# A hybrid decoder layer on one core: an earlier start of a pair's mixing, token-wise squares, sums on VectorE, ordered sigmoids

## The chip, the core and the metric

The kernel runs on one core of one Trainium2 chip. The core has a matrix engine (TensorE, PE in the rows; PEld is its weight load), VectorE (DVE), ScalarE (ACT), GpSimd (POOL) and SyncE (SP), whose queue issues the DMA transfers of this kernel. The metric is the device time of one execution in microseconds (us), lower is better. A profiled execution also leaves a trace, with a span from the first to the last instruction.

## The reference, cut to what matters

One layer over 2048 prompt tokens and 8 x 8 sample tokens, width 1024:

```python
h = rmsnorm(x, norm_mix_w)                     # input norm
rq, rk, rv, rg, hq, hf, hi, hg = split(h @ w_in)
rq, rk = rotary(rq, pos), rotary(rk, pos) * 128 ** -0.5
o_r = head_rmsnorm(chunk_gla(rq, rk, rv, log_gamma)) * silu(rg)      # 4 retention heads
f = lb + (1 - lb) * sigmoid(hf)
o_h = head_rmsnorm(chunk_gla(silu(hq) * c, 1 - f, hi, log(f))) * silu(hg)  # 4 HGRN heads
x = x + concat(o_r, o_h) @ w_out
x = x + square(relu(rmsnorm(x) @ w_up)) @ w_down
y = rmsnorm(x)
```

`chunk_gla` is a causal gated recurrence, computed chunk by chunk: scores inside a chunk, times decays that come from running sums of log f, plus the state carried over. Outputs are y and the states after the last token.

## The kernel before, in words

Tokens lie along the free dimension. They go through the layer in three groups: group 0 (64 sample and 512 prompt tokens, 576 columns), groups 1 and 2 (768 prompt tokens each). The kernel first mixes group after group, and then does the feed-forward of the three groups. Products are made from float32 values split into a rounded high part (a ScalarE copy, L298 for weights, L434 in `cut`) and a low remainder (a VectorE subtraction, L312, L435), three matmuls for each product.

**Pairs.** Inside a group `mix` goes over four pairs, each a retention head with an HGRN head. A pair has a forget block f and a query block q of the HGRN head, a rotary query block rq and key block rk of the retention head (`project`, `project_quads`), then the value blocks (`values`, L1007), and two gate blocks, which are made one pair later, for the last pair at once (`gates`, `gates_quad`). Groups 1 and 2 make two blocks at a time by a Strassen-like scheme of seven products of 12 matmuls (`quad`, L828): the results are collected in two PSUM tiles, ScalarE copies the first, third and fifth product out (L834, L838, L843), and VectorE adds the others (L816). One sum of two SBUF halves (L841) is on GpSimd. The fifth product accumulates onto the bank of the first, so PE has to wait for the copy of L834 before it.

Rotary (L885 to L889): four half-height ScalarE copies swap halves, VectorE multiplies by the cosine, GpSimd by the sine (L888), VectorE adds. Sigmoids of two blocks are taken together in `sigmoids` (L852): ScalarE needs the sigmoid table for them, and the table set that holds both logarithm and exponential is asked for behind them (L854). The request for the set is kept in program order, the two sigmoids are not.

**Mixing.** `mixer` writes a pair's chunk work into an agenda by due times: logarithms (L1137, L1138), running sums on VectorE (L1143), then, for block widths 64, 32, ... 2, exponents on GpSimd (L1159, L1160), exponentials on ScalarE (L1164), products on VectorE (L1170), and matmuls (corners L1241 for the wide blocks, L1184 for narrow ones). Then come transposes (L1298, L1112), outputs and states (L1368 to L1383) and the head norm with the gate (`gate_norm`, L443, L444, L1460 to L1468). Due times count from t0, in ticks: every two matmuls of a projection block and every three of a value block are a tick, and at each tick what is due is written into the program. In the kernel before, t0 is the tick at which rq and rk are done, or the end of the mixing before it.

**Order.** The order of instructions on each engine is decided by the scheduler of the tile framework, which works from the order of writing and its own estimate of times; `keep_in_program_order` pins an instruction, `high_priority` draws it forward. So an instruction's place follows its due time only roughly.

**Output projection and input norm.** `out_proj` multiplies the heads of three pairs with their weights and adds the input (`residual`, L1510, eight blocks), then adds the last pair (L1553). Beside it, `norm_in` of the next group runs by due times: load x block by block, square on ScalarE (L622), add on VectorE (L625), column sums on PE (L604, L605), reciprocal root (L443, L444), load x again, scale it (L655), round it (L657) and subtract (L661).

**Sums of weights.** During group 0 `plan_quads` makes the weights of the seven products: per set of blocks four loads of 128 x 512, four sums on GpSimd (L364), high parts on ScalarE (L369), low parts on VectorE (L372), eight stores; ten sets, the first at tick 110 and then every 80 ticks. During groups 1 and 2 `plan_sums` does the like for the feed-forward in buffers named raw (L1525); there are four of these, which the weight loads also use.

Of the kernel before, what the change touches and what calls it, by code (L numbers as in the profile page):

```python
# [9 lines left out]
F32 = mybir.dt.float32  # L10
# [209 lines left out]
class Kernel:  # L220
# [133 lines left out]
    def plan_quads(self, start, each):  # L354
# [8 lines left out]
        def make(x, name, a, op, b, into):  # L363
            order(nc.gpsimd.tensor_tensor(out=x[into], in0=x[a], in1=x[b], op=op))  # L364
            x[name] = x[into]
# [97 lines left out]
    def build(self):  # L463
        nc, tc, I = self.nc, self.tc, self.I
        with ExitStack() as ctx:
# [46 lines left out]
            for ns, p0, n in GROUPS:  # L512
                g = type("G", (), {})()
                g.i, g.ns, g.p0, g.n, g.T, g.off = len(gs), ns, p0, n, ns + n, off
                off += g.T
                nch = n // C
                first = nch // 2
                g.pieces = [(0, g.T)] if g.T <= 512 else [(0, g.T // 2), (g.T // 2, g.T)]
                g.segs = [list(range(first)), list(range(first, nch))]
                g.scaled = bool(gs)  # L520
                gs.append(g)
            nc.scalar.dma_start(vec, I["vec"])
# [25 lines left out]
            self.mix(gs[1])  # L548
            self.out_proj(gs[1], 1, lambda: self.norm_in(gs[2], pace=6))
            self.plan_sums(sums[NQ:], at)  # L550
# [76 lines left out]

    def norm_in(self, g, start=False, pace=5):

# [19 lines left out]

        def squares(kb):  # L650
            g.sq = self.add_square(g, g.sq, self.x_block(g, kb), nc.vector)

# [49 lines left out]
        if start:  # L702
# [30 lines left out]
    def mix(self, g):  # L733
        nc = self.nc
# [7 lines left out]
        for p in range(H):  # L742
# [3 lines left out]
            if g.scaled and p == 0:  # L746
                self.plan_sides(g)
            (self.project_quads if g.scaled and p else self.project)(g, p, b)
            end = self.mixer(g, p, b, max(self.now, end))
            if g.scaled and p == H - 1:  # L750
                self.gates_quad(g, b)
                for i in range(H - 1):
                    self.later(1 + 14 * i, self.get_heads, g, i)
                    self.later(16 + 14 * i, self.cut_heads, g, i)
            self.values(g, p, b)
            prev = b
        if g.scaled:
            return
        for p in range(H - 1):
            self.later(2 + 18 * p, self.cut_heads, g, p)  # L760
        self.gates(g, prev)

    def plan_sides(self, g):
# [46 lines left out]
    def quad(self, g):  # L810
# [6 lines left out]
        for k, (A, B) in enumerate(QUAD):  # L817
# [21 lines left out]
            elif k == 3:  # L839
                add(s[:, two], ps, s[:, two])  # L840
                nc.gpsimd.tensor_tensor(out=Q[:, two], in0=s[:, two], in1=s[:, one], op=ALU.add)  # L841
            elif k == 4:
# [7 lines left out]
    def sigmoids(self, *pairs):  # L850
        for out, src in pairs:
            self.nc.scalar.activation(out, src, AF.Sigmoid)  # L852
        with self.tc.high_priority():
# [12 lines left out]

    def project_quads(self, g, p, b):

# [12 lines left out]
        self.later(5, forget)  # L881
        self.later(8, lambda: nc.gpsimd.tensor_tensor(out=z[:, :T], in0=z[:, :T], in1=sgq[:, :T], op=ALU.mult))
        for key, r in zip(("rq", "rk"), self.quad(g)):
            xs = self.get()
# [4 lines left out]
            self.later(9, lambda r=r, xs=xs: nc.vector.tensor_tensor(out=r[:, :T], in0=r[:, :T], in1=xs[:, :T], op=ALU.add))  # L889
            b[key] = r  # L890

    def block(self, g):
# [30 lines left out]

    def project(self, g, p, b):
        nc, T = self.nc, g.T
# [38 lines left out]
        self.later(5, lambda: eng.tensor_tensor(out=self.v2(hq, g), in0=z, in1=self.v2(sgq, g), op=ALU.mult))  # L964

        for key in ("rq", "rk"):
            if not start or key == "rk":
# [5 lines left out]
            self.later(9, lambda q=q, xs=xs: nc.vector.tensor_tensor(out=q[:, :T], in0=q[:, :T], in1=xs[:, :T], op=ALU.add))  # L973
            b[key] = q

    def values(self, g, p, b):
# [145 lines left out]
    def mixer(self, g, p, b, t0):  # L1122
# [5 lines left out]
        q, k, f = b["q"], b["k"], b["f"]  # L1128
        rq, rk = b["rq"], b["rk"]
        cols = [slice(n0 + C * c, n0 + C * (c + 1)) for c in range(n)]  # L1130
# [979 lines left out]
```

## Time and profile before

| | |
|---|---|
| Median of three runs | 2606.51 us (2604.39 to 2615.03) |
| Profiled execution | 2608.76 us, its span 2607.0 us |
| PE busy | 2488.5 us, 95% |
| DVE, ACT, POOL busy | 1933.8, 1335.7, 490.3 us |
| Mean granted PE clock | 0.982 |

How to read it: windows give for each stretch its length and the busy time of each engine with its count of instructions, the granted PE clock, the busy share of the DMA engines and GB/s. A row of waits names who waited for whom, the total in us, the times, and the longest. A group row ends with the busy time and the mean ns of one instruction, then the idle time ahead of it. A busy PE row can contain overlap, and a matmul is slower while the granted clock is 0.5.

### The profile page before, as it was taken

To read this page: it belongs to the slowest core of one execution; us is meant where nothing else is said; L and a number is where in the kernel's file an instruction comes from. 1 tells how busy PE (TensorE), PEld (TensorE's weight loads), DVE (VectorE), ACT (ScalarE), POOL (GpSimd) and SP (SyncE) were. 2 spreads that over 40 slices of the span, in tenths; PEclk is the share of its full clock that TensorE was granted. 3 is DMA by queue.
4 is the path that set the end of the run, shared out by engine and by line. 5 is a ranking of instruction groups with operands and counts; after the bars stand their busy time and mean duration, and the time that the engine had idled before them with its cause. 6 is when DMAs were issued, how large, how long until landed. Compare 5 with 4: busy or idle time off the path is not lost.

```text
span 2607.0 us, 41951 instructions
## 1 busy us (share of the span) xinstructions
PE 2488.5 (95%) x16280; PEld 2451.7 (94%) x16280; DVE 1933.8 (74%) x2567; ACT 1335.7 (51%) x1796; POOL 490.3 (19%) x373
## 2 busy tenths in 40 slices
PE   8999879999989999998999999999999999999998
PEld 8989778988979998888999999999999999999998
DVE  6777778665577756656587799875699868668977
ACT  6665644456554454653464555544454435445443
POOL 6455521453340234523000000000000000000000
PEclk9999989999999999998999999999999999999999
DMA  7778688676866687685586876676666546766553
GB/s 262 256 266 278 217 282 309 235 267 235 289 234 206 250 299 252 243 288 211 197 279 217 274 242 203 211 228 217 215 238 212 172 154 218 244 197 223 181 172 108
DMA packets 226952, 605.16 MB, mean 232 GB/s; under 512 B 23489, under 2 KB 65089, under 8 KB 226754
## 3 DMA queue, kind: packets, MB, share of 16 engines
q1 hardware_dynamic: 226610, 602.47, 67.5%
q8 instruction: 128, 2.10, 0.3%
q14 instruction: 70, 0.57, 0.1%
q10 hardware_dynamic: 144, 0.02, 0.0%
HBM read 448.51 MB, written 152.83 MB: 231 GB/s over the span
## 4 chain that ended last, share of the span: by engine, by line
PE 59%; DVE 2%; POOL 2%; issue 2%; ACT 1%; DVEq 0%; POOLq 0%; ACTq 0%
PE pf L1495 25%; PE pj L1495 24%; PE pj L828 4%; PE pj L427 3%; PE pjv L1007 1%; POOL slab L1160 1%; PE mm L1184 1%; POOL slab L1159 1%; PE po L1370 0%; PE mm L1376 0%; PE po L1368 0%; POOL slab L888 0%; DVE slab L889 0%; DVE lo L312 0%; DVE slab L1143 0%
## 5 line engine op out<-in xcount | busy, mean ns | idle before, releaser
L298 ACT CAST hi<-raw 128x1024 fp32r<-128x1024 f32 x392 | 411.9, 1051 | 604.7 <-PE pj L1495 224.8
L1495 PE MATMUL pf<-slab,hi 128*128 128x384 f32 (+1 forms) x2768 | 652.7, 321 | 0.0
L1495 PE MATMUL pj<-slab,hi 128*128 128x384 f32 (+1 forms) x2608 | 618.2, 322 | 0.0
L312 DVE TENSOR_TENSOR lo<-raw,hi 128x1024 fp32r<-128x1024 f32 x392 | 485.6, 1239 | 114.5 <-ACT hi L298 112.3
L1495 PEld LDWEIGHTS pf<-slab,hi 128*128 128x128 f32 x2768 | 480.4, 188 | 0.1
L1495 PEld LDWEIGHTS pj<-slab,hi 128*128 128x128 f32 x2608 | 454.0, 188 | 0.0
L1495 PE MATMUL pf<-slab,lo 128*128 128x384 f32 (+1 forms) x1384 | 443.6, 320 | 0.0
L1495 PE MATMUL pj<-slab,lo 128*128 128x384 f32 (+1 forms) x1304 | 419.6, 322 | 0.6 <-DVE lo L312 0.6
L427 PE MATMUL pj<-slab,hi 128*128 128x288 f32 (+1 forms) x1792 | 364.2, 319 | 15.1 <-DVE slab L1510 10.3
L828 PE MATMUL pj<-slab,unit 128*128 128x384 f32 x1680 | 348.2, 352 | 25.1 <-ACT slab L834 13.2
L828 PEld LDWEIGHTS pj<-slab,unit 128*128 128x128 f32 x1680 | 294.8, 194 | 30.0 <-ACT slab L834 15.1
L427 PEld LDWEIGHTS pj<-slab,hi 128*128 128x128 f32 x1792 | 290.8, 191 | 18.9 <-issue 9.7
L1495 PEld LDWEIGHTS pf<-slab,lo 128*128 128x128 f32 x1384 | 260.2, 188 | 0.0
L1495 PEld LDWEIGHTS pj<-slab,lo 128*128 128x128 f32 x1304 | 245.1, 188 | 0.9 <-DVE lo L312 0.8
L427 PE MATMUL pj<-slab,lo 128*128 128x288 f32 (+1 forms) x896 | 214.0, 319 | 1.1 <-DVE lo L312 1.1
L1007 PE MATMUL pjv<-hi,slab 128*128 128x256 f32 x1024 | 207.1, 294 | 2.7 <-DVE slab L971 2.7
L1007 PEld LDWEIGHTS pjv<-hi,slab 128*128 128x128 f32 x1024 | 170.1, 198 | 4.6 <-DVE slab L971 3.0
L1588 DVE TENSOR_TENSOR slab<-slab 128x768 fp32r<-128x768 f32 (+1 forms) x192 | 166.7, 885 | 8.8 <-ACT slab L1584 4.5
L1584 ACT CAST slab<-slab 128x768 fp32r<-128x768 f32 (+1 forms) x192 | 144.8, 778 | 53.1 <-DVE slab L1595 42.5
L427 PEld LDWEIGHTS pj<-slab,lo 128*128 128x128 f32 x896 | 153.0, 191 | 1.9 <-DVE lo L312 1.5
L1007 PE MATMUL pjv<-lo,slab 128*128 128x256 f32 x512 | 148.3, 290 | 0.0
L1164 ACT ACTIVATE slab<-slab 128x768 f32<-128x768 f32 (+2 forms) x72 | 56.1, 780 | 136.9 <-POOL slab L1160 85.1
(261 smaller groups left out, 3494.2 us busy)
## 6 DMA issues: line engine op xcount, KB each, us to landing
raw<-w SPq DMA_DIRECT2D x264, 512.0 KB, 4.5
ld<-x SPq DMA_DIRECT2D x64, 384.0 KB, 4.0
slab<-u SPq DMA_DIRECT2D x64, 384.0 KB, 4.8
u<-ld SPq DMA_DIRECT2D x60, 384.0 KB, 4.3
ld<-in SPq DMA_DIRECT2D x28, 384.0 KB, 3.9
slab<-w SPq DMA_DIRECT2D x40, 256.0 KB, 5.1
slab<-u SPq DMA_DIRECT2D x32, 288.0 KB, 4.2
u<-ld SPq DMA_DIRECT2D x30, 288.0 KB, 3.3
```

Source lines behind the costliest of these rows:

```text
L298: self.nc.scalar.copy(hi, raw)
L312: self.nc.vector.tensor_tensor(out=lo, in0=self.second.pop(j), in1=hi.bitcast(F32), op=ALU.subtract)
L427: self.nc.tensor.matmul(pj[:, i, :T2], w, a[:, c0:c1], start=j == 0 and q == 0, stop=j == n - 1 and q == 2)
L828: nc.tensor.matmul(ps, w[:, c], a, start=first and kb == q == 0, stop=kb == KB // 2 - 1 and q == 2, skip_group_check=not first)
L1007: nc.tensor.matmul(pj[:, i * 256:(i + 1) * 256], a[:, s:s + C], ww, start=kb == 0 and q == 0, stop=kb == KB - 1 and q == 2)
L1159: nc.gpsimd.tensor_tensor(out=D4[:, :, 0, :], in0=mid, in1=K4[:, :, 0, :], op=ALU.subtract)
L1160: nc.gpsimd.tensor_tensor(out=D4[:, :, 1, :], in0=B4[:, :, 1, :], in1=mid, op=ALU.subtract)
L1164: nc.scalar.activation(x["dd", w][:, a:T], x["dd", w][:, a:T], AF.Exp)
L1184: nc.tensor.matmul(ps[:, j], qk[:, cols[c]], second(qk[:, cols[c]]), start=True, stop=True)
L1495: self.nc.tensor.matmul(*a, **k)
L1584: self.nc.scalar.copy(hi[:, :g.T], B[name][:, :g.T])
L1588: self.nc.vector.tensor_tensor(out=lo[:, :g.T], in0=B[name][:, :g.T], in1=hi.bitcast(F32)[:, :g.T], op=ALU.subtract)
```

## The change

In groups 1 and 2 a pair's mixing begins 16 ticks behind the f and q blocks and no longer behind rq and rk; the due times of what needs rq and rk move back by 4 ticks, and those of the two diagonal sums by 6. In group 0 mixing begins where it did. The two sigmoids of `sigmoids` are pinned in program order, so both stand ahead of the request for the next table set.

The input norm of the next group begins earlier, behind the gate blocks of the last pair (ahead of those in group 0). It reads x once with a chunk's tokens on the partitions (a new input `xt`, the same values laid out anew) into the raw buffers, six loads of 128 x 1024, squares each with the sum along the row (`accum_out`), takes the reciprocal root of a 128 x 6 tile, writes this to a row in DRAM, and reads the row back for all partitions. The eight squares and seven additions in x's column layout, the column sums on PE and the roots of full width go. The scaling of the eight blocks starts with the first residual block, every 18 ticks.

The four sums of each set of `plan_quads` move from GpSimd to VectorE, and the sets run from tick 100 every 66 ticks. The sum of two halves in `quad` moves to VectorE too.

```diff
-            order(nc.gpsimd.tensor_tensor(out=x[into], in0=x[a], in1=x[b], op=op))
+            order(nc.vector.tensor_tensor(out=x[into], in0=x[a], in1=x[b], op=op))
...
-            self.plan_quads(110, 80)
-            self.mix(gs[0])
-            self.out_proj(gs[0], 1, lambda: self.norm_in(gs[1], pace=6))
+            self.plan_quads(100, 66)
+            rest = self.mix(gs[0], gs[1])
+            self.out_proj(gs[0], 0, rest)
...
-        def squares(kb):
-            g.sq = self.add_square(g, g.sq, self.x_block(g, kb), nc.vector)
+        def squares(c):
+            t = self.wp.tile([P, WT], F32, tag="raw", name="raw", bufs=NRAW)
+            nc.sync.dma_start(t, self.I["xt"][:, (g.first + c) * WT:(g.first + c + 1) * WT])
+            self.later(14, lambda: nc.scalar.activation(t, t, AF.Square, accum_out=g.sq[:, c:c + 1]))
+
+        def factors():
+            n = g.n // C
+            self.rsqrt(g.sq[:, 8:8 + n], g.sq[:, :n], g.sq[:, 8:8 + n], self.eps, D)
+            row = self.dp.tile([1, T], F32, name=f"r{g.i}")
+            with nc.allow_non_contiguous_dma("a column for each chunk"):
+                nc.sync.dma_start(row[0].rearrange("(c p) -> p c", p=P), g.sq[:, 8:8 + n])
+            g.rs = self.get()
+            nc.sync.dma_start(g.rs[:, :T], row.to_broadcast([P, T]))
...
-        for kb in range(KB):
-            self.later(pace * kb, squares, kb)
-        t0 = pace * KB
-        self.later(t0 + 4, split)
-        self.later(t0 + 12, factor)
+        g.sq = self.small.tile([P, 16], F32, tag="sq", name="sq")
         g.h = [None] * KB
-        for k in range(KB):
-            self.later(t0 + 20 + 9 * k, scaled, k)
-        self.later(t0 + 92, tables)
+        for c in range(g.n // C):
+            self.later(5 * c, squares, c)
+        self.later(5 * (g.n // C) + 12, factors)
+
+        def rest():
+            for kb in range(KB):
+                self.later(4 + pace * kb, scaled, kb)
+            self.later(2 + pace * KB, tables)
+        return rest
...
-            (self.project_quads if g.scaled and p else self.project)(g, p, b)
-            end = self.mixer(g, p, b, max(self.now, end))
+            def begin(ticks=16):
+                return self.mixer(g, p, b, max(self.now + ticks, end))
+
+            if g.scaled:
+                end = (self.project_quads if p else self.project)(g, p, b, begin)
+            else:
+                self.project(g, p, b)
+                end = begin(0)
...
-                nc.gpsimd.tensor_tensor(out=Q[:, two], in0=s[:, two], in1=s[:, one], op=ALU.add)
+                nc.vector.tensor_tensor(out=Q[:, two], in0=s[:, two], in1=s[:, one], op=ALU.add)
...
     def sigmoids(self, *pairs):
         for out, src in pairs:
-            self.nc.scalar.activation(out, src, AF.Sigmoid)
+            self.tc.keep_in_program_order(self.nc.scalar.activation(out, src, AF.Sigmoid))
...
+        behind = 4 if g.scaled else 0
...
-        at(67, own, 0)
-        at(70, own, 1)
+        at(73 if g.scaled else 67, own, 0)
+        at(76 if g.scaled else 70, own, 1)
...
-            at(46 + 4 * sg, ret_scores, sg)
-            at(60 + 4 * sg, turn, "ktr", rk, sg, C_KS)
-        at(60, ret_queries)
+            at(46 + behind + 4 * sg, ret_scores, sg)
+            at(60 + behind + 4 * sg, turn, "ktr", rk, sg, C_KS)
+        at(60 + behind, ret_queries)
```

More of the change, by code (lines that the diff above doesn't have):

```diff
@@ L520, in build @@
                 g.scaled = bool(gs)
+                g.first = (p0 - GROUPS[1][1]) // C
                 gs.append(g)
@@ L626, in add_square, with norm_in @@
         return acc
-    def norm_in(self, g, start=False, pace=5):
+    def norm_in(self, g, start=False, pace=18):
         nc, T = self.nc, g.T
@@ L754, in mix @@
                     self.later(16 + 14 * i, self.cut_heads, g, i)
+                nxt = nxt and self.norm_in(nxt)
             self.values(g, p, b)
@@ L882, in project_quads @@
         self.later(8, lambda: nc.gpsimd.tensor_tensor(out=z[:, :T], in0=z[:, :T], in1=sgq[:, :T], op=ALU.mult))
+        end = begin()
         for key, r in zip(("rq", "rk"), self.quad(g)):
@@ L890, in project_quads @@
             b[key] = r
+        return end
     def block(self, g):
@@ L964, in project @@
         self.later(5, lambda: eng.tensor_tensor(out=self.v2(hq, g), in0=z, in1=self.v2(sgq, g), op=ALU.mult))
+        end = begin and begin()
         for key in ("rq", "rk"):
@@ L974, in project @@
             b[key] = q
+        return end
     def values(self, g, p, b):
```

17 lines of the change are left out of this document (10 added, 7 removed).

## The prediction

> **What bounds the kernel now.** I read the stages first: busy time of each engine in windows cut at the groups. Columns: window, length, then PE, PEld, DVE, ACT and POOL busy (instructions), granted clock, DMA share, GB/s.
>
> ```profile
> 0.00:330.00 330.00, 301.57 (x2296) 289.42 (x2297) 244.18 (x414) 208.11 (x342) 183.15 (x175) 0.98 0.74 257
> 330.00:445.00 115.00, 95.80 (x590) 91.53 (x589) 88.14 (x127) 53.55 (x81) 18.51 (x14) 0.88 0.85 295
> 470.00:780.00 310.00, 281.90 (x1939) 273.82 (x1938) 195.69 (x318) 166.90 (x242) 130.82 (x83) 0.97 0.75 262
> 895.00:1222.00 327.00, 297.92 (x2039) 289.21 (x2038) 207.43 (x333) 174.59 (x251) 139.36 (x90) 0.95 0.70 250
> 1265.00:2607.00 1342.00, 1332.53 (x8299) 1330.39 (x8297) 1069.27 (x1183) 654.03 (x774) 0.00 (x0) 1.00 0.64 212
> ```
>
> PE bounds everything. The last window is the feed-forward: 1332.5 of 1342 us busy at full clock, and the change does not touch it. So all that can be won lies in front of it. PE is idle there for 28.4 us in group 0, 19.2 us in the passage to group 1, 28.1 us in group 1 and 29.1 us in group 2; the windows left out lose little. There is a second loss: the granted clock is under 1 where PE has idled. Taken over whole windows that is at most 0.03 x 310 = 9.3 us in group 1, 0.05 x 327 = 16.4 us in group 2 and 0.12 x 115 = 13.8 us in the passage.
>
> The view of waits, PE's longest, says whom PE waits for:
>
> ```profile
> PE mm L1241 <- DVE slab L1170: 17.4, 6, 4.1
> PE pj L828 <- ACT slab L834: 13.2, 2, 6.6
> PE mm L604 <- ACT slab L434: 10.5, 6, 1.8
> PE pj L427 <- DVE slab L1510: 10.3, 3, 8.1
> PE pj L828 <- DVE slab L816: 10.1, 4, 3.4
> ```
>
> L828 exists in groups 1 and 2 only, and L1510 only in output projections. So four of these rows, 51.2 us, are nearly the 57.2 us of idle PE in the two groups. They are the target; each is followed below to its cause.
>
> **Sigmoids in order.** Table loads on ScalarE, by groups:
>
> ```profile
> L444 ACT ACT_TABLE_LOAD x24 | 30.8, 1283 | 0.4
> L852 ACT ACT_TABLE_LOAD x20 | 25.7, 1283 | 60.7 <-DVE slab L816 60.7
> L443 ACT ACT_TABLE_LOAD x18 | 23.1, 1283 | 0.3
> L854 ACT ACT_TABLE_LOAD x14 | 18.0, 1283 | 0.2
> L1137 ACT ACT_TABLE_LOAD x6 | 7.7, 1283 | 0.1
> ```
>
> L854 restores the set with both logarithm and exponential, so L443, L444 and L1137 should need no loads. They need 48, because in six of the fourteen pairs of sigmoids the request stands between the two, and the set is then wrong until the next request. With both sigmoids pinned, L852 needs 14 loads and the others none; the built program of the changed kernel has just these. That removes 54 x 1.283 = 69.3 us from ScalarE, which is far from full (166.9 of 310 us), so the sum counts only what lies ahead of a PE wait. The longest is at the gate blocks of the last pair (rows of the timeline: start, length, instruction, idle time ahead of it); ScalarE:
>
> ```profile
> 1166.00 0.83 ACT L885 COPY slab<-slab 64x768 f32<-64x768 f32 x1 [1.09 <-DVE slab L816]
> ...
> 1169.39 1.28 ACT L1137 ACT_TABLE_LOAD   x1
> 1170.69 1.03 ACT L1137 ACTIVATE slab<-slab,lb,a 128x768 f32<-128x768 f32 x1
> ...
> 1172.54 0.56 ACT L443 ACTIVATE slab<-mm,eps 128x384 f32<-128x384 f32 x1
> 1173.12 1.28 ACT L444 ACT_TABLE_LOAD   x1
> 1174.85 0.46 ACT L834 COPY slab<-pj 128x384 f32<-128x384 f32 x1
> ```
>
> and PE there:
>
> ```profile
> 1175.36 7.27 PE L828 MATMUL pj<-slab,unit 128*128 128x384 f32 x24 [6.56 <-ACT slab L834]
> 1184.13 4.46 PE L828 MATMUL pj<-slab,unit 128*128 128x384 f32 x24 [1.50 <-DVE slab L816]
> ```
>
> The copy that PE needs stands behind the rotary copies, a load, two logarithms (1170.69 to 1172.54), a root and another load. Both loads (2.6 us) go, and the logarithms (1.9 us) move 26 ticks ahead: 4.5 us of the 6.56. It happens twice; with a little less traffic besides I take 10 us of the 13.2 (bounds 0 and 13.2). After the wait 24 matmuls take 7.27 us, the next 24 only 4.46: this is the cold clock, 2.8 us more, counted under Clock.
>
> The Trainium skill, "ScalarE: Activation LUTs", section What ACT_TABLE_LOAD costs, puts a switch at 1283 ns plus a drain of 1380 ns, 2.66 us in all. Here the logarithm starts 0.02 us after its load ends, and the load right behind the last copy, so the trace bears out the first figure and not the second. By the skill's figure 54 switches would be 144 us of ScalarE, and the two of this stretch 5.3 us instead of 2.6; the whole wait would go, 3 us more in the sum.
>
> **Earlier mixing.** From the start of the logarithms to the first corners, in a middle pair (ScalarE, POOL, then PE):
>
> ```profile
> 1079.68 1.03 ACT L1137 ACTIVATE slab<-slab,lb,a 128x768 f32<-128x768 f32 x1
> 1084.92 3.88 POOL L1160 TENSOR_TENSOR slab<-slab 128x384 f32<-128x384 f32 x1 [3.74 <-DVE slab L1143]
> 1091.77 0.53 PE L1241 MATMUL mm<-slab 128*64 128x64 f32 x6 [4.12 <-DVE slab L1170]
> 1119.90 6.49 PE L828 MATMUL pj<-slab,unit 128*128 128x384 f32 x36
> ```
>
> and ScalarE at the sigmoids that end two blocks:
>
> ```profile
> 1124.37 1.58 ACT L852 ACTIVATE slab<-slab 128x768 f32<-128x768 f32 x2
> ...
> 1127.26 0.83 ACT L434 CAST slab<-slab 128x768 fp32r<-128x768 f32 x1
> ```
>
> The chain takes 12.1 us, and 2.6 us of this is that one L1160 took 3.88 instead of its mean 1.295 us (row below), while VectorE worked on rotary and sums. A tick is two matmuls, 2 x 6.49 / 36 = 0.36 us, so 26 ticks are 9.4 us. But the built program also draws the corners forward: they now stand behind 72 of the 84 matmuls of the rq/rk blocks, 13.0 us behind f and q. The chain from there is a load, two sigmoids and the next load, 1.28 + 1.58 + 1.28 = 4.1 us, and then 9.5 us without the slow exponent or 12.1 with it: 13.6 to 16.2 us. So a wait of 0.6 to 3.2 us stays at each of six places; I take 1.4, so 9 of the 17.4 us go (bounds -2 and 14). rq and rk are now done 26 ticks behind t0, and the first scores that read them are due 50 behind it: 24 ticks, 8.6 us, lie between for the four copies and the sums of the rotary part; in the rows above the copies take 3.4 us. That covers it, and I cost the move of 4 ticks at nothing; if the cover failed, PE would wait for L889 at L1298, some 2 us a pair.
>
> L604 waits for L434, which in these rows is held up by the sigmoids of the gate blocks. With t0 26 ticks earlier this cut is due in the middle of the gate blocks, ahead of the sigmoids. I take 9 of 10.5 us (bounds 0 and 10.5); what falls there instead are the outputs and states, which need no ScalarE.
>
> **Sums on VectorE.** The groups that move, and the nearest rows for their price:
>
> ```profile
> L364 POOL TENSOR_TENSOR slab<-slab 128x512 f32<-128x512 f32 x40 | 61.3, 1533 | 41.1 <-DVE slab L435 27.7 <-DMA slab<-w 10.6 <-issue 1.5
> L841 POOL TENSOR_TENSOR slab<-slab 128x384 f32<-128x384 f32 x20 | 25.7, 1285 | 165.7 <-DVE slab L816 107.2 <-issue 58.5
> L1160 POOL TENSOR_TENSOR slab<-slab 128x384 f32<-128x384 f32 (+2 forms) x72 | 93.2, 1295 | 38.7 <-DVE slab L1143 36.4 <-DMA n731A<-lo 2.2
> L372 DVE TENSOR_TENSOR slab<-slab 128x512 fp32r<-128x512 f32 x40 | 36.8, 922 | 0.9 <-POOL slab L364 0.8
> L816 DVE TENSOR_TENSOR slab<-pj,slab 128x384 f32<-128x384 f32 x80 | 44.5, 556 | 70.3 <-PE pj L828 70.3
> L625 DVE TENSOR_TENSOR slab<-slab 128x768 f32<-128x768 f32 (+1 forms) x17 | 18.8, 1107 | 2.4 <-ACT slab L622 1.9
> ```
>
> L841 blocks POOL's queue for 107.2 us while it waits for L816, and the exponents stand behind it; in the last pair they then hold up L1170 and, behind that on VectorE, the L816 that PE awaits. On VectorE it costs 20 x 0.556 = 11.1 us, hidden by VectorE's slack there (195.7 of 310 us busy). I take 8 of the 10.1 us of PE waits (bounds 0 and 10.1).
>
> L364 costs VectorE 40 x 0.922 = 36.9 us in place of 61.3 us of POOL. The sets end at tick 100 + 9 x 66 + 78 = 772 instead of 908, so it all lands in group 0, where VectorE has 244.2 of 330 us; it comes to 281, or 85%. PE then waits more often for VectorE. Bounds: VectorE's rows get shorter as POOL's go (gain 10 us), or half of the new work reaches PE (loss 18 us). I take a loss of 5 us.
>
> **Squares by tokens.** Of L625, 14 go (15.5 us of VectorE), twelve longer squares on ScalarE stand for sixteen, at no cost while ScalarE is busy for 53.6 of the passage's 115 us (were they alone on the path, a microsecond each), and the sets of weights no longer run in the passage. That passage is where L1510 waited 8.1 us at once. Scaling every 18 ticks instead of 9 also thins VectorE there. I take 8 of the 10.3 us (bounds 0 and 10.3). New is the way through DRAM: scaling is due 10 ticks, 3.6 us, behind the roots, and the row is 768 elements of four bytes. The nearest is L694, a read of single elements:
>
> ```profile
> DMA to landing us min/median/max: 4.1/4.1/4.1
> raw<-w SPq DMA_DIRECT2D x264, 512.0 KB, 4.5
> ```
>
> The write and the read back follow each other, so 8 to 9 us pass, and for about 5 us VectorE stands at the first scaling with L1510 behind it, SP at the read with weights behind it. Two PSUM tiles and two weight blocks of lead cover most. I take 1.5 us for each of two passages, loss 3 (bounds 0 and 10).
>
> **Clock.** The four rows are won to 36 of 57 us of idle PE in the two groups, 63%. Of the 25.7 us of lost clock a good half falls on busy PE: 25.7 x 0.63 x 0.6 = 10 us.
>
> **Sum.** -10 - 9 - 9 - 8 - 8 - 10 + 5 + 3 = -46 us. The profiled execution took 2608.76 us, span 2607.0; that is 2.3 us above the median of 2606.51. So 2608.8 - 46 - 2.3 = 2560.5 us for the median.
>
> **The rivals.** (1) Everything named clears: 51.2 us of the four rows, 10.3 of L1510 and 20 of clock, with group 0 unharmed: 2606.5 - 81 = 2525 us. For it speaks that each row has a cause that the change touches; against it that the corners were drawn forward.
> (2) The waits move and do not go: the corners and the last pair wait for the chain as before, and only L604 (9), L816 (8) and a little clock (4) are won, less 8 of new cost: 2593 us. For it speaks that the scheduler places instructions by an estimate which it has missed six times by 3 us.
> (3) Slower: the raw buffers. Squares hold these, four in all, for a landing (4.5 us) and a square, and SP issues in order; the weights of the output projection load through the same buffers behind them. If each of six weight blocks in both passages came 5 us later than PE needs it, 60 us would be added: 2620 us. It decides once a weight is more than its lead of two blocks late; a block of 36 matmuls lasts 36 x 0.18 = 6.5 us, so the delay has to pass 13 us. Against it: six loads take some 10 us at the 300 GB/s that these windows reach.
>
> One rule of the Trainium skill speaks against the change: "DMA: Bandwidth & Descriptors", section Specifications, says that below 512 B the DMA engine reads, modifies and writes, and the norm row's elements have four bytes. By it the way through DRAM would cost its upper bound, and the sum would be -39 us. The 4.1 us of L694, as long as a load of 512 KB, agrees that small elements are slow; no row here shows a write of them.
>
> **Chances.** My forecast 0.62, rival 1 0.17, rival 2 0.14, rival 3 0.07. A change under 0.5% (13 us, below 2593.5) can't be told from none. Rival 2 lies on that bound and is split: faster 0.62 + 0.17 + 0.07 = 0.86, same 0.07, slower 0.07. The range, 2525 to 2592, reaches to rival 1 and to the near edge of rival 2, and leaves out under 2 in 10.
>
> **What would show it.** Right: no table loads at L443, L444 and L1137; PE's waits for L434 and L834 gone from the head of the list; idle PE in the two group stages near 10 us each and their clock at 0.98; VectorE at 85% in group 0. Wrong: PE waiting for scaled blocks or weights in a passage, more idle PE in group 0 than 34 us, or the corners' row as long as before.

## The result: slower by 1.45%

The changed kernel takes 2646.68 us (median of three runs, 2645.48 to 2646.96) against 2606.51 us; the ratio is 1.0145 (95% interval 1.0109 to 1.018). Its profiled execution has a span of 2643.7 us at a mean granted clock of 0.972, where the kernel before had 2607.0 us at 0.982. The forecast was 2560.5 us (2525 to 2592): a gain of 46 us, where a loss of 40 us came.

The waits of PE after the change (who waited for whom, total us, times, longest):

```profile
PE mm L1326 <- DVE slab L914: 27.3, 6, 9.0
PE pj L852 <- DVE slab L840: 15.2, 12, 2.5
PE pj L427 <- ACT slab L1048: 8.3, 2, 6.2
PE po L1398 <- DVE S L1411: 7.7, 2, 7.4
PE mm L1326 <- DVE slab L1000: 6.8, 2, 4.4
PE mm L606 <- DVE slab L435: 6.5, 1, 6.5
...
PE pj L427 <- DVE slab L1539: 4.4, 4, 2.2
...
PE pj L852 <- ACT slab L858: 2.4, 5, 0.6
...
PE mm L1269 <- DVE slab L1198: 1.3, 1, 1.3
```

The lines have moved by 24 to 29: L852 is the quad product (L828 before), L840 its addition (L816), L858 the copy of its first product (L834), L1539 the residual (L1510), L1269 the corners (L1241), L912 and L914 are the rotary cosine product and sum (L887, L889), L1326 the retention scores (L1298), L1198 the product of exponents (L1170). The three rows that the change aimed at hardest, L1241 for L1170, L828 for L834 and L604 for L434, 41.1 us together, are gone from the head (1.3 and 2.4 us are left of the first two, and no row of the third). In their place stand the scores, which wait for the rotary sums in all eight pairs of the two groups: 34.1 us with the row of pair 0 (L1000). The windows, cut as before (columns as there):

```profile
0.00:330.00 330.00, 298.55 (x2194) 286.04 (x2195) 248.41 (x434) 203.58 (x340) 130.94 (x141) 0.94 0.77 264
470.00:780.00 310.00, 280.69 (x1857) 267.86 (x1857) 194.54 (x315) 124.54 (x205) 110.74 (x73) 0.95 0.66 241
780.00:895.00 115.00, 107.02 (x673) 105.85 (x672) 71.06 (x105) 51.47 (x75) 1.85 (x1) 0.95 0.79 251
```

PE issues 102 instructions fewer in the first 330 us and 82 fewer in 470 to 780 us, at a lower clock, and 780 to 895 us, which lost nothing before, loses 8 us. The pages of the two profiles, before and after, set the waits in proportion:

```profile
PE 2488.5 (95%) x16280; PEld 2451.7 (94%) x16280; DVE 1933.8 (74%) x2567; ACT 1335.7 (51%) x1796; POOL 490.3 (19%) x373
PE 2514.8 (95%) x16272; PEld 2467.2 (93%) x16272; DVE 1946.6 (74%) x2609; ACT 1263.0 (48%) x1742; POOL 394.6 (15%) x313
```

PE's idle time, its span less its busy time, grows by only 10.4 us, from 118.5 to 128.9: the waits that went pay for most of the new ones. The other 26.3 us are busy time, with eight matmuls fewer. That fits the granted clock, which is 0.010 lower over some 2640 us (26 us, an estimate). The start times of the matmuls give the length of each stage (worked out from the timelines of both kernels):

| stage | before | after | difference |
|---|---|---|---|
| group 0, to its first residual block | 313.2 | 330.8 | +17.6 |
| its output projection, to group 1's first block | 102.1 | 94.0 | -8.1 |
| group 1: pair 0, blocks and values | 57.8 | 71.4 | +13.6 |
| first to last quad product | 280.3 | 281.8 | +1.5 |
| to its first residual block | 26.1 | 22.4 | -3.7 |
| its output projection | 79.5 | 87.8 | +8.3 |
| group 2: pair 0 | 56.3 | 69.0 | +12.7 |
| first to last quad product | 281.8 | 281.8 | 0.0 |
| last quad product to the feed-forward | 103.7 | 98.4 | -5.3 |
| feed-forward | 1297.3 | 1297.3 | 0.0 |

In pair 0 the length is not all loss. PE has 422 and 423 matmuls there in place of 357, work that the earlier start brings forward, most of it from behind the last quad product; its idle time grows only from 3.5 to 7.8 us in group 1 and from 2.3 to 5.4 us in group 2.

So three parts of the change could each be blamed: mixing (pair 0, and quads that win nothing), sums on VectorE (group 0), squares by tokens (the projection of group 1).

### The profile page after: what moved, and what is told of

The parts are those of the page before. It is cut to its first block, busy times and chain, and to the rows that moved or that the text cites. A ratio compares the mean times of both kernels' runs of the same rounds, so it can differ in the third digit from the quotient of the medians.

```text
span 2643.7 us, 41710 instructions
## 1 busy us (share of the span) xinstructions
PE 2514.8 (95%) x16272; PEld 2467.2 (93%) x16272; DVE 1946.6 (74%) x2609; ACT 1263.0 (48%) x1742; POOL 394.6 (15%) x313
## 4 chain that ended last, share of the span: by engine, by line
PE 75%; DVE 9%; DMA 5%; issue 4%; ACT 4%; POOL 3%; SPq 1%; DVEq 0%; ACTq 0%; POOLq 0%
PE pf L1524 24%; PE pj L1524 23%; PE pj L427 10%; PE pj L852 7%; PE pjv L1035 4%; DMA ld<-x 1%; PE mm L1212 1%; DMA r<-sq 1%; POOL slab L1187 1%; POOL slab L913 1%; PE mm L1326 1%; PE po L1398 1%; PE mm L1404 1%; PE po L1396 1%; POOL slab L1188 1%
## 5 line engine op out<-in xcount | busy, mean ns | idle before, releaser
L312 DVE TENSOR_TENSOR lo<-raw,hi 128x1024 fp32r<-128x1024 f32 x392 | 484.7, 1237 | 113.8 <-ACT hi L298 108.4
L427 PE MATMUL pj<-slab,hi 128*128 128x288 f32 (+1 forms) x1792 | 368.3, 323 | 16.0 <-ACT slab L1048 8.3
L852 PE MATMUL pj<-slab,unit 128*128 128x384 f32 x1680 | 339.5, 349 | 20.0 <-DVE slab L840 15.2
L852 PEld LDWEIGHTS pj<-slab,unit 128*128 128x128 f32 x1680 | 292.3, 192 | 32.0 <-DVE slab L840 20.2
L427 PEld LDWEIGHTS pj<-slab,hi 128*128 128x128 f32 x1792 | 295.6, 194 | 20.4 <-ACT slab L1048 8.7
L427 PE MATMUL pj<-slab,lo 128*128 128x288 f32 (+1 forms) x896 | 217.6, 322 | 0.8 <-DVE lo L312 0.7
L427 PEld LDWEIGHTS pj<-slab,lo 128*128 128x128 f32 x896 | 156.5, 194 | 1.7 <-DVE lo L312 1.3
```

Of the source, the lines that this page charges most:

```text
L312: self.nc.vector.tensor_tensor(out=lo, in0=self.second.pop(j), in1=hi.bitcast(F32), op=ALU.subtract)
L427: self.nc.tensor.matmul(pj[:, i, :T2], w, a[:, c0:c1], start=j == 0 and q == 0, stop=j == n - 1 and q == 2)
L852: nc.tensor.matmul(ps, w[:, c], a, start=first and kb == q == 0, stop=kb == KB // 2 - 1 and q == 2, skip_group_check=not first)
```

## The experiments

Times are medians, ratios are to the kernel before, run beside each.

| kernel | us | ratio (95%) |
|---|---|---|
| only_sigmoids | 2613.5 | 1.0019 (1.0009 to 1.0029) |
| only_mixing | 2641.3 | 1.0123 (1.0106 to 1.0140) |
| only_sums | 2608.1 | 0.9995 (0.9986 to 1.0005) |
| only_tokens | 2616.0 | 1.0030 (1.0018 to 1.0042) |
| no_mixing | 2622.6 | 1.0053 (1.0038 to 1.0068) |
| no_mixing_order | 2623.5 | 1.0058 (1.0037 to 1.0080) |
| after_start_late | 2639.6 | 1.0118 (1.0101 to 1.0135) |
| after_scores_12 | 2608.7 | 1.0002 (0.9992 to 1.0012) |
| after_scores_late | 2610.3 | 1.0002 (0.9992 to 1.0012) |
| after_scores_only (computes something else) | 2632.2 | 1.0091 (1.0076 to 1.0106) |
| after_turn_early | 2627.6 | 1.0058 (1.0038 to 1.0077) |
| mixing_scores_late | 2626.9 | 1.0069 (1.0054 to 1.0085) |
| only_query_sums | 2607.2 | 0.9994 (0.9983 to 1.0004) |
| tokens_rows | 2601.8 | 0.9966 (0.9952 to 0.9980) |
| late_rows | 2590.4 | 0.9935 (0.9918 to 0.9951) |
| late_rows_12 | 2590.5 | 0.9914 (0.9896 to 0.9932) |
| late_rows_28 | 2598.4 | 0.9968 (0.9952 to 0.9984) |
| late_rows_pool | 2590.9 | 0.9936 (0.9921 to 0.9951) |

### Each part alone on the kernel before

Each of these holds the lines of the change's diff that belong to one part, and nothing else: the pinned sigmoids; the start of the mixing with its due times; L364, L841 and `plan_quads(100, 66)`; the input norm.

> The kernel before with both sigmoids kept in order and nothing else. The prediction's own step: 54 table loads less, PE's wait L828 <- L834 falls from 13.2 to some 3 us, with its share of clock about 12 us less: 2594 us. Rival: ScalarE is off the path, pinning only delays other work behind the sigmoids: 2606 +- 6 us. If the loss of the whole change (+40 us) came from here, this kernel would be slower than 2620 us.

> The kernel before with the mixing of a pair begun behind its forget and query blocks (16 ticks), the own columns at 73 and 76, the retention scores 4 ticks later, and nothing else. The prediction's own step: 18 us of waits and some clock less: 2585 us. Theory A: the early start lets the planner place the retention scores ahead of their rotary sums, PE waits some 9 us there where the trace of the changed kernel shows L1326 <- L914 at two or three places, and pair 0 gets 13 us longer in groups 1 and 2: 2625 us or more, with that wait in the list. If the loss comes from elsewhere: under 2600 us.

> The kernel before with the weights' sums (L364, quads planned at 100 and 66) and the query sums (L841) on VectorE and nothing else. The prediction's own step: -8 +5 us: 2603 us. Theory B: VectorE is filled in group 0, whose time up to the residual grows by 17 us as in the changed kernel: 2616 to 2624 us, with 313 us to the residual becoming 325 or more.

> The kernel before with the input norm's squares by whole tokens, the factors through a DRAM row, scaling every 18 ticks, and nothing else. The prediction's own step: -8 +3 us: 2601 us. Theory C: VectorE stands at the first scaled block until the row is back, the output projection of group 1 grows by 8 us and pair 0 of groups 1 and 2 starts on blocks that are not yet scaled: 2614 to 2630 us.

The mixing alone costs 1.23%, some 32 us; the four add up to 1.67%, near the 1.45% of the whole. Theory A is borne out in size, and its wait is in the list (L1309 for L897, the scores for the rotary sum: 13.2 us in six). The 9 us at one place are not there, for the longest of these waits is 2.6 us; and that pair 0 is longer by 14.1 and 10.1 us is in large part work brought forward, as above. Theory C holds in size (0.30%, some 8 us) and in place: the output projection of group 1 grows from 79.5 to 90.3 us. Theory B fails: the sums make group 0 longer by 13.7 us up to the residual, but 5.3 us come back in the passage, and the rest behind it. The sigmoids alone win nothing, although their loads go as forecast.

The mixing alone shows a second thing. ScalarE in group 2, behind the f and q blocks of the first middle pair (L841 and L845 are the copies of a quad's first and third product there, L835 is the quad product, L859 the sigmoids, L1149 a logarithm):

```profile
989.26 1.28 ACT L859 ACT_TABLE_LOAD   x1
...
991.42 1.28 ACT L443 ACT_TABLE_LOAD   x1
...
993.68 1.28 ACT L444 ACT_TABLE_LOAD   x1
...
995.52 1.28 ACT L443 ACT_TABLE_LOAD   x1
...
998.33 1.28 ACT L444 ACT_TABLE_LOAD   x1
...
1000.16 1.28 ACT L1149 ACT_TABLE_LOAD   x1
1001.46 1.03 ACT L1149 ACTIVATE slab<-slab,a,na 128x768 f32<-128x768 f32 x1
1002.39 0.46 ACT L845 COPY slab<-pj 128x384 f32<-128x384 f32 x1
```

The logarithms now come among the copies that the products of the rotary blocks need, and the loads that unordered sigmoids cause stand between; PE waits for L841 and L845 (7.3 and 8.4 us). So these two parts seem to hang together, which is put in numbers below.

### Where the mixing loses

```diff
# after_scores_late (20), after_scores_12 (12)
-        behind = 4 if g.scaled else 0
+        behind = 20 if g.scaled else 0
```
```diff
# after_start_late
-                return self.mixer(g, p, b, max(self.now + ticks, end))
+                return self.mixer(g, p, b, max(self.now + (ticks and (42 if p else 48)), end))
```

> The changed kernel with the retention scores, their keys' turn and the queries' decay 16 ticks later still (behind 20 in place of 4 in the scaled groups); the start of the mixing stays early. Theory A (what the early mixing costs is that the scores are placed ahead of their rotary sums): the wait L1326 <- L914, 27.3 us in the changed kernel, falls under 5 us and the time falls by 20 to 27 us, to 2620 to 2627 us. Rival: the rotary chain and VectorE are late as a whole; the wait moves to the next reader or comes back in the blocks of the next pair: 2636 us or more.

> The changed kernel with the mixing's due times moved back behind the rotary blocks (42 ticks in the quads, 48 in pair 0, in place of 16); the order of the code and the other three parts stay. Theory A and its rival both: the early start itself costs some 30 us, so this is 2612 to 2620 us, the sum of the three other parts measured alone on the kernel before (+4.0 -1.4 +6.5 us, about 2619). If the loss of the mixing lies in the later own columns or in the order of the code and not in the start, it stays at 2640 us.

> The changed kernel with all three steps 8 ticks later in place of 16 (behind 12). The rotary chain behind the last block took 12.7 us there (560.0 to 572.7 us), and the first score stood 3.4 us behind the block's end, 9.1 us too early; 8 ticks are 2.9 us. If the loss goes with the lateness, tick by tick: 2630 to 2636 us. If a step decides (the scores then leave the values' first third): within 4 us of 2610 us.

Eight ticks decide: with the scores, the turn of the keys and the decay of the queries 8 or 16 ticks later, the time falls by 1.43%, 37 us, more than theory A expected (20 to 27 us). With 12 ticks PE's idle time falls by 19.6 us and its busy time by 18.9, and the clock rises from 0.972 to 0.983 (0.979 with 20 ticks). From the first to the last quad product there are then 268.1 and 266.5 us (12 ticks) in place of 281.8 in both groups. In the changed kernel, this is VectorE, then PE, behind the last quad block of the first middle pair, whose last product is added at 560.00:

```profile
560.00 0.56 DVE L840 TENSOR_TENSOR slab<-pj,slab 128x384 f32<-128x384 f32 x1 [1.51 <-PE pj L852]
562.36 0.96 DVE L912 TENSOR_TENSOR slab<-slab,ld 128x768 f32<-128x768 f32 x1 [1.80 <-ACT slab L911]
565.02 1.61 DVE L914 TENSOR_TENSOR slab<-slab 128x768 f32<-128x768 f32 x1 [1.70 <-POOL slab L913]
566.55 2.55 DVE L912 TENSOR_TENSOR slab<-slab,ld 128x768 f32<-128x768 f32 x1
569.03 2.15 DVE L1198 TENSOR_TENSOR slab<-slab 128x384 f32<-128x384 f32 x1
571.11 1.65 DVE L914 TENSOR_TENSOR slab<-slab 128x768 f32<-128x768 f32 x1
```
```profile
572.81 0.80 PE L1326 MATMUL mm<-slab 128*128 128x128 f32 x2 [8.94 <-DVE slab L914]
```

The chain from the block to the second sum takes 12.8 us. The product of exponents of the early mixing stands inside it on VectorE, and GpSimd works beside it. But the chain was long before: in the kernel before, it took 11.2 us at this place (VectorE, the last addition and the second sum):

```profile
540.70 0.55 DVE L816 TENSOR_TENSOR slab<-pj,slab 128x384 f32<-128x384 f32 x1
...
550.98 0.93 DVE L889 TENSOR_TENSOR slab<-slab 128x768 f32<-128x768 f32 x1
```

There 138 value matmuls stood ahead of the scores, and PE did not wait. In the changed kernel only 26 do, so PE idles 8.9 us. With 12 ticks the same place reads:

```profile
567.98 1.66 DVE L914 TENSOR_TENSOR slab<-slab 128x768 f32<-128x768 f32 x1
```
```profile
569.79 0.91 PE L1326 MATMUL mm<-slab 128*128 128x128 f32 x6 [1.30 <-DVE slab L914]
```

The scores now stand behind 96 value matmuls, and PE waits 1.3 us, though the chain is no shorter (555.94 to 569.64 us). In the second middle pair the changed kernel had 85 matmuls ahead of them and waited 2.0 us. The due time gives 72 matmuls (24 ticks of three), so the scheduler drew the scores 46 forward in one pair and put them 13 back in the next. With 12 and 20 ticks they stand where they are due in both, behind 96 and 120. The tick-by-tick reading is refuted by the 12 ticks, which do as well as 20.

The late start was expected by both theories to restore 2612 to 2620 us, and did not. Two runs close in on it:

```diff
# no_mixing_order: after_start_late, and
-        behind = 4 if g.scaled else 0
+        behind = 0 if g.scaled else 0
-        at(73 if g.scaled else 67, own, 0)
+        at(67, own, 0)
...
-        at(76 if g.scaled else 70, own, 1)
+        at(70, own, 1)
```

> The changed kernel with the earlier mixing undone whole: sigmoids in order, sums on VectorE and squares by tokens stay. If the parts add up as the four measured alone did (+4.0 -1.4 +6.5 us): 2617 to 2621 us, and the changed kernel with only the start moved back, 2639.6 us, then carries 20 us that belong to the late own columns and the order of the code. If that kernel shows a collision of the other three parts with each other, this one is above 2632 us too.

> The changed kernel with the start moved back (42 and 48 ticks) and the own columns and the scores at their old ticks: of the mixing's edit only the order of the code is left. If the order alone costs nothing: 2620 to 2625 us, as with the mixing undone whole, and the 17 us of the kernel with the late start belong to the own columns and scores that stand 4 to 6 ticks later beside an old start. If the order of the code costs them: 2637 us or more.

no_mixing leaves the whole mixing edit out. Without it the other three parts give 1.0053, so the mixing as written costs 0.92%, 24 us, beside them, and with its scores at 12 or 20 ticks it wins 0.51%, 13 us. The order of the code costs nothing (1.0058). The 0.6% between that kernel and the late start belong to own columns and scores that come 4 to 6 ticks later beside the old start: due times that only fit the early start. Through which wait they cost it isn't shown; the list there is led by the quad products, which wait for their copy (L852 for L858, 19.6 us) and their addition (L852 for L840, 18.3 us).

```diff
# after_scores_only
-            at(46 + behind + 4 * sg, ret_scores, sg)
+            at(46 + behind + (16 if g.scaled else 0) + 4 * sg, ret_scores, sg)
# after_turn_early: after_scores_late, and
-            at(60 + behind + 4 * sg, turn, "ktr", rk, sg, C_KS)
+            at(60 + (4 if g.scaled else 0) + 4 * sg, turn, "ktr", rk, sg, C_KS)
```

> The changed kernel with the retention scores alone 16 ticks later; the keys' turn and the queries' decay stay where the change has them. If the scores on TensorE carry the loss: 2608 to 2614 us, as with all three moved (2610.3). If the turn or the decay carry part of it, because TensorE waits for the same rotary sums at the transposes that now come first: 2620 us or more, with a wait for L914 at L1140.

> The changed kernel with the scores and the decay of the queries 16 ticks later (20 in place of 4), the turn of the keys left at 4. If the scores carry the loss: 2607 to 2613 us, as with all three moved. If the turn of the keys, whose transposes read the same rotary sums, carries part of it: 2618 us or more, with TensorE waiting at L1140.

after_scores_only moves `ret_scores` alone by 16 ticks, so that the decay of the queries comes ahead of the scores: they read decayed queries, which is another computation. It decides nothing. after_turn_early moves scores and decay and leaves the keys' transposes (turn) at 4. The wait for L914 is gone, but a new one takes its place, 17.1 us in four waits (PE):

```profile
569.61 0.66 PE L1212 MATMUL mm<-slab 128*128 128x64 f32 x2 [7.09 <-DVE slab L1198]
```

Here matmuls of a narrow width (L1212) stand behind the same 26 value matmuls, and wait for a product of exponents that was made late on VectorE. So it is not the scores as such: in both kernels what the scheduler draws into the 13 us behind the rotary blocks waits there, while VectorE and GpSimd are behind with rotary and exponents together. Of the 37 us, moving the scores and the decay won 0.87%, some 23 us, and the turn the other 0.56%, 15 us. Why the scheduler goes as far forward as 26 matmuls stays open.

Next, only_mixing with behind 20:

> The kernel before with the earlier mixing alone, but the retention scores 20 ticks later in place of 4 (the mixing alone as written took 2641.3 us). The scores' place was worth 36 us in the changed kernel. If it is worth as much without the other parts: 2603 to 2610 us, with L1309 <- L897 (13.2 us) gone. If the mixing needs the sigmoids in order, because the nine table loads that stood among its logarithms and the blocks' copies remain: 2615 to 2630 us, with L835 waiting for L841 and L845.

With the late scores but unordered sigmoids the mixing still costs 0.69%; L1309 for L897 (13.2 us) is gone, but L835 still waits for L841 and L845 (7.3 and 7.1 us). Add the sums (-0.05%) and the tokens (+0.30%), and 0.94% would be due; with ordered sigmoids as well it measured 0.02%. So the order of the sigmoids, worth nothing alone, is worth some 0.9%, 24 us, beside an early mixing, if the other parts add. No run has these two parts alone; that parts add is borne out by sigmoids, sums and tokens without the mixing, 0.44% as a sum and 0.53% as measured.

### The way of the row through DRAM

In the kernel with the squares by tokens alone: SP at the write and the read of the row, then VectorE and PE.

```profile
781.79 0.38 SPq L661 DMA_DIRECT2D r<-sq  x1
...
794.25 0.32 SPq L663 DMA_DIRECT2D slab<-r  x1
```
```profile
799.99 1.02 DVE L667 SCALAR_TENSOR_TENSOR ld<-ld,vec,slab 128x768 f32<-128x768 f32 x1 [13.76 <-DMA slab<-r]
```
```profile
801.93 0.69 PE L606 MATMUL mm<-slab,ones_r 128*128 128x384 f32 x1 [10.12 <-DVE slab L435]
```

The write of 768 single elements took so long that SP could issue the read only 12.5 us later; VectorE stood 13.8 us at the first scaling, and the remainder that PE's column sum needs stood behind it. The next run turns the tile of factors first:

```diff
-            with nc.allow_non_contiguous_dma("a column for each chunk"):
-                nc.sync.dma_start(row[0].rearrange("(c p) -> p c", p=P), g.sq[:, 8:8 + n])
+            ps, flat = self.mm(P), self.get()
+            nc.tensor.transpose(ps[:n], g.sq[:, 8:8 + n], self.ident)
+            nc.scalar.copy(flat[:n, :P], ps[:n])
+            nc.sync.dma_start(row[0].rearrange("(c p) -> c p", p=P), flat[:n, :P])
```

> The squares by whole tokens alone, as measured, but the factors are turned on TensorE first, so that the row is written to DRAM as six runs of 512 bytes in place of 768 single elements. In the trace of the squares alone the write of single elements was issued at 781.8 us, the read behind it at 794.2, VectorE stood 13.8 us. Theory C1 (the single elements are slow): the write takes 2 to 3 us, VectorE's wait at the first scaling falls to 4 us, the time to 2603 to 2608 us. Theory C2 (any way through DRAM takes this long): the wait stays above 10 us and the time at 2616 us.

```profile
773.32 0.28 SPq L663 DMA_DIRECT2D r<-slab  x1
...
777.64 0.32 SPq L665 DMA_DIRECT2D slab<-r  x1
```
```profile
782.71 1.02 DVE L669 SCALAR_TENSOR_TENSOR ld<-ld,vec,slab 128x768 f32<-128x768 f32 x1 [4.85 <-DMA slab<-r]
```

Theory C1 holds: 4.3 us from write to read, VectorE stands 4.9 us, the gap on PE is down from 10.1 to 1.2 us, and the squares by tokens win 0.34%, some 9 us, where with single elements they cost 0.30%.

### The sums, and all that pays together

```diff
# only_query_sums: the kernel before, and
-                nc.gpsimd.tensor_tensor(out=Q[:, two], in0=s[:, two], in1=s[:, one], op=ALU.add)
+                nc.vector.tensor_tensor(out=Q[:, two], in0=s[:, two], in1=s[:, one], op=ALU.add)
```

> The kernel before with the query sums (L841) on VectorE and nothing else; the weights' sums L364 stay on GpSimd at the old pace. Both sums together measured -1.4 us, with group 0 longer by 13.6 us up to the residual, its passage shorter by 5.3, and 8 us won behind it. If L364 is what costs group 0: 2599 to 2603 us with L828 <- L816 under 9 us. If the gain behind group 0 came from L364 leaving GpSimd: 2607 to 2610 us.

> The changed kernel with both remedies: the scores 20 ticks later (2610.3 us alone) and the factors turned before the write to DRAM (14 us under the squares with single elements). If they add: 2594 to 2598 us, under the kernel before. If the passage's wait only uncovers another: 2603 us or more.

> The same with the weights' sums L364 back on GpSimd at the old pace; the query sums stay on VectorE. Group 0 up to the residual was 15 us longer, its passage 6.5 shorter, with L364 on VectorE. If that is L364's cost and nothing pays it back: 8 us under the kernel that has it on VectorE, 2586 to 2590 us. If GpSimd's 61 us in group 0 and the passage cost as much through stretched VectorE instructions: the same time within 3 us.

only_query_sums moves L841 alone: 0.9994, the same as both moves, and like them not clear of noise. late_rows is the changed kernel with behind 20 and the turned factors: 0.9935, so the remedies add by their ratios (1.0002 x 0.9966 / 1.0030 = 0.9938), though the time is under the range expected. late_rows_pool differs from it in `plan_quads(110, 80)` and L364 on GpSimd, and takes the same time (0.9936), the second of the two cases expected. By stages, L364 on VectorE makes group 0 longer by 16.4 us up to the residual (328.9 against 312.5), the passage shorter by 10.2 (84.0 against 94.2) and pair 0 of group 1 shorter by 6.9: paid back where the sets no longer run.

> The kernel with both remedies (2590.4 us), the scores another 8 ticks later (behind 28). If the cover is complete at 20: the same time within 4 us. If scores still wait: down to 2582 us. If they now crowd the outputs of the pair: 2595 us or more.

> Both remedies with behind 12. If 12 ticks are enough beside the other remedy too: 2588 to 2594 us, as with 20 (2590.4). If the scores still wait where the passage no longer holds VectorE: 2596 us or more.

28 ticks are worse than 20 (0.9968 against 0.9935; whether the scores crowd the outputs was not followed up), 12 are as good. The version with both remedies beats both kernels: 2590.5 us with 12 ticks (0.9914). Its first waits on PE, with all lines two further down:

```profile
PE pj L854 <- DVE slab L842: 18.5, 10, 4.3
PE pj L427 <- ACT slab L1050: 7.8, 2, 6.4
PE pjv L1033 <- DVE slab L1000: 5.1, 2, 3.4
```

## Why the prediction was wrong

**The step that failed** is in Earlier mixing: "24 ticks, 8.6 us, lie between for the four copies and the sums of the rotary part; in the rows above the copies take 3.4 us. That covers it, and I cost the move of 4 ticks at nothing; if the cover failed, PE would wait for L889 at L1298, some 2 us a pair." The prediction held the 3.4 us of the copies alone against the cover. The whole chain took 12.8 us: copies, two cosine products, two sine products on GpSimd and two sums, with mixing between them; and in the kernel before it already took 11.2 us, so that 8.6 us could not cover it even where the due times hold. Nor was the cover 8.6 us: in the worst pair it was 26 value matmuls, some 3 us. The price, put at nothing, was 27.3 us in six waits: 2.0 and 2.7 us in two of the three pairs of each group, near the 2 us named for a failed cover, and 9.0 us in the first. The prediction had noticed that the built program draws the corners forward, and didn't look where it puts the scores. With 8 ticks more the rest of the step was right in kind: the mixing wins 13 us beside the other parts, of the 18 claimed.

Most of what the prediction aimed at did go: in the changed kernel L1241 for L1170 fell from 17.4 to 1.3 us, L828 for L834 from 13.2 to 2.4, L604 for L434 left the list, and L1510 fell from 10.3 to 4.4; only the row of L816 grew, from 10.1 to 15.2. For new waits the sum held only 5 us for VectorE and 3 us for the row. The scores are the largest of these, but not the only ones: without their loss the kernel is back at the time before (1.0002), and with the row turned as well it is some 22 us faster, not 46.

**Sigmoids in order (-10).** The loads went as said: 14 remain at the sigmoids, none at the logarithms and roots.

```profile
L876 ACT ACT_TABLE_LOAD x14 | 18.0, 1283 | 32.1 <-DVE slab L840 32.0
L878 ACT ACT_TABLE_LOAD x14 | 18.0, 1283 | 0.2
```

But alone that took L828 <- L834 only from 13.2 to 9.1 us: behind the rotary copies the logarithms and a root still stood ahead of the copy. The prediction counted on their coming earlier, which is the other part's doing; with both the row fell to 2.4 us. A removed cost was booked to one part that takes two. Why the time alone rose by 0.19% isn't shown. With the sigmoids alone ScalarE's busy time fell from 1335.7 to 1266.9 us, by 68.8, near 54 x 1.283 = 69.3 us. By the 2.66 us each of the Trainium skill's "ScalarE: Activation LUTs", What ACT_TABLE_LOAD costs, it would be 144 us, an estimate; no run shows the half of it that is the drain.

**Sums on VectorE (-8 +5).** The sum of terms was near, -3 against -1.3 us (0.05%, not clear of noise), by wrong terms: alone, L828 <- L816 fell only from 10.1 to 8.4 us, and in the changed kernel VectorE's busy time in the first 330 us did not go to 281 (85%) but to 248.4: other rows of VectorE shortened (L372 from 922 to 799 ns), and PE got less far in this time.

**Squares by tokens (-8 +3).** The price of the row was mis-sized: the prediction took 1.5 us a passage, with 10 in all as the upper bound; the runs showed 10.1 us of one PE wait in group 1's passage alone, and +0.30% in all. The row it came from, L694, is a read; the write of single elements lands in 10.0 to 12.4 us. The rule that the prediction weighed, of the Trainium skill's "DMA: Bandwidth & Descriptors", Specifications (below 512 B the DMA engine reads, modifies and writes), speaks for the right end: with runs of 512 bytes the read could be issued 4.3 us behind the write, in place of 12.5. The gain of 8 us is borne out by tokens_rows (9 us).

**Clock (-10).** The term took the lost clock to shrink in step with the idle time that is won. It did not keep step: idle PE grew by 9% (118.5 to 128.9 us), while the clock fell from 0.982 to 0.972, which is over half as much lost again (0.028 in place of 0.018). With the scores 8 ticks later it is 0.983. Which waits cost the clock most isn't shown.

**The rivals.** Rival 3, slower by the raw buffers, came out on the right side, at 2620 us, by luck: no run shows its mechanism, and PE's wait for weights (L427 for L312, their low parts) is 0.7 us in the changed kernel, 1.1 before. Rival 2 named what happened in the quads, where the waits moved and the length stayed (+1.5 and 0.0 us), but not the waits for the rotary sums or the loss in the passage.

## What to carry to other kernels

When work is started earlier, list for each of its inputs the whole chain that makes it, across all engines and at the lengths that the rows have while the engines are busy together, and look in the built program how many matmuls really stand ahead of the first reader: due times in the source do not say it. Measure the parts of a joint change alone and left out: here the sigmoids' order was worth nothing alone and, by the sum of the parts, 0.9% beside the early start. A small reduction that goes through DRAM should be turned so that its write is contiguous.

## What the hardware showed that was not expected

In the kernel with the squares by tokens alone, a DMA write of 768 elements of four bytes took 11.2 us to land in the median (two writes), two and a half times a load of 512 KB (rows: KB each, median us to landing):

```profile
raw<-w SPq DMA_DIRECT2D x264, 512.0 KB, 4.5
...
r<-sq SPq DMA_DIRECT2D x2, 3.0 KB, 11.2
```

And a VectorE product of two SBUF operands took 2.7 times as long where it began while GpSimd was at work. In the rows shown of the changed kernel L912 runs in 0.96 us at 562.36 and in 2.55 us at 566.55. GpSimd there:

```profile
562.40 2.58 POOL L913 TENSOR_TENSOR slab<-slab,ld 128x768 f32<-128x768 f32 x1 [6.19 <-ACT slab L911]
...
565.78 2.51 POOL L1219 TENSOR_TENSOR slab<-slab 128x768 f32<-128x768 f32 x1
568.25 2.52 POOL L913 TENSOR_TENSOR slab<-slab,ld 128x768 f32<-128x768 f32 x1
```

The short one began 0.04 us ahead of GpSimd's product, the long one amid another. L912's mean is 1767 ns in the changed kernel, where L887 had 952 before. In the kernel before it was the sum L889 that showed it: 2.59 us where it began at 545.69 while GpSimd worked, and 0.93 us where it began at 550.98 while GpSimd stood. That GpSimd is the cause is read from rows that lie together; no run takes it away alone.
